# Expert tables split into fp16 halves during the mixers' heads and kept in DRAM: loaded ready, the first table by transposing DMAs, with the key roles exchanged

## The chip, the cores and the metric

The kernel runs on one core of one Trainium2 chip. The metric is the device time of one execution in microseconds (us); lower is better. Times of the kernel before are a median of 3 runs. The profile is one further execution, taken by the hardware profiler on the same program.

## The reference

One layer with two pre-norm sub-layers over 1024 latent tokens of 1024 channels; a prefix of 256 context tokens only feeds the start states. The first sub-layer is a pair of linear-attention mixers (8 HGRN heads and 4 GLA heads, both directions). The second is PEER, a product-key expert network of 128 x 128 = 16384 single-neuron experts:

```
q  = (tok @ wq).reshape(-1, 8, 2, 128)
s1 = einsum("nhd,kd->nhk", q[:, :, 0], k1)
s2 = einsum("nhd,kd->nhk", q[:, :, 1], k2)
v1, i1 = top_k(s1, 16)
v2, i2 = top_k(s2, 16)
top_s, top_c = top_k(v1[..., :, None] + v2[..., None, :], 16)
expert = i1[top_c // 16] * 128 + i2[top_c % 16]
gate = softmax(top_s)
act = gelu(einsum("pd,ped->pe", x, u[expert]))
out = einsum("pe,ped->pd", gate * act, v[expert])
```

Each token picks 16 experts in each of 8 heads. `u` and `v` are tables of 16384 rows of 1024 fp32 numbers (64 MiB each).

## The kernel before, in words

**Arithmetic.** TensorE works in fp16. Every large product is made of three: both operands are split into a high and a low fp16 half (`split`, lines 90 to 93: one ACT instruction writes the high half, one DVE instruction the low half), and `mm3` (lines 95 to 100) multiplies high by high, high by low and low by high, all added up in PSUM. All these matmuls show up under line 99; they are told apart by their output: `pj` (projections of the mixers), `pv` (their values by token), `pb` and `pso` (merge and output projection), `pq` (queries of the experts' keys), `ph` (u times the tokens), `pe` (activations times v).

**Order of the work.** The program is written out in full. A scheduler of the language orders each engine's instructions when the program is built: each engine then runs its own list strictly in order, and waits at the head of the list where an input is late. DMAs are issued from the lists of SP (`ld`: nearly all loads), ACT (`st_`: the stores) and POOL (the indirect gathers), in the same way.

**Stages.** First the modulation and norm, up to about 70 us of the profile. Then the mixers' *heads* (lines 299 to 682): `hg_proj`/`hg_scan` for 8 heads, `gla_proj`/`gla_scan` for 4, each loading 128 weight columns at a time through `slab` (line 165; three fp32 buffers `w32`), with the projections of the next head issued ahead of the scan of this one. In a scan DVE runs a chain of states (`R`, line 433) that PE feeds and reads. `merge_gate` and `modulation` (lines 611 and 621) fill in and close the heads. Then the merge and output projection (752 to 852), and then PEER.

**PEER.** Two of the eight blocks of 128 tokens do not go through all experts: `gathering` (line 864) fetches their chosen rows of u and v by indirect DMAs from POOL (line 892), 512 of them, and DVE uses each row (lines 871 and 876). The other 768 tokens go through all 16384 experts, in 128 tiles of 128. Tile `e` holds the experts `i * 128 + e`, so `i`, the first key, runs over the partitions. For each tile:

- `u_load` (line 902) loads 128 rows of u (512 KB fp32, `un`, two buffers);
- `u_turn` (line 907) transposes them with 8 PE transposes in fp32 against the identity into PSUM (`put`), ACT writes the high half (line 917) and a scaled fp32 copy (`uf`, line 919), POOL subtracts to the low half (line 920); the result `uT` has two buffers;
- `u_act` (line 925) multiplies with the tokens (48 matmuls into two PSUM tiles `ph`) and ACT takes the gelu;
- `weigh` (line 1078) multiplies with the gates on DVE and splits; `v_tile` (line 1087) loads 128 rows of v (`vn`, two buffers) and splits them on ACT and DVE (lines 92 and 93);
- `out_unit` (line 1094) multiplies four tiles' worth of activations with v (`pe`) and DVE adds the result to `acc`.

48 of the 128 tiles are *early* (line 123): their `u` part runs during the product-key stage (`prep`, line 1025: `route`, `choosing`, `gate_block`) and is kept in DRAM (`act_d`). The other 80 are *live*, and run in the expert stage, between 2880 and 4510 us of the profile. The gates are made by `gate_block` (line 995) from one-hot rows and kept in DRAM as `G_d`, with the first key ahead of the second. Two marks hold DVE's and POOL's order: `vmark` puts the use of a gathered row behind the last named DVE instruction (line 869), `pace` puts a gather's issue behind the last POOL subtraction of `u_turn`:

```
G.tensor_tensor(out=lo, in0=uf, in1=hi, op=ALU.subtract)
with tc.issue_after(pace[0].ins):
    G.indirect_dma_start(out=row, out_offset=None, in_=src[0], ...)
```

Of the kernel before, what the change touches and what calls it, by code (L numbers as in the profile page):

```python
# [8 lines left out]
F32 = mybir.dt.float32  # L9
# [9 lines left out]
P = 128  # L19
# [12 lines left out]
# powers of two that keep the low halves of split operands out of fp16's subnormals  # L32
# [30 lines left out]
AHEAD = 4  # L63


@with_exitstack
def tile_layer(ctx: ExitStack, tc: tile.TileContext, x, c, ctxt, c_ctx, ada_w, ada_b, norm_mix_g,
# [58 lines left out]
    # activations by feature: the mixers' input first, the experts' input later  # L126
# [5 lines left out]
    def rms_cols(tiles, pl, tag):  # L132
        """1 / rms of each row of the tiles"""
# [9 lines left out]
    def norm_T(tiles, ss, dst, sc, sh, pl, pp, tag, rows_of=None):  # L143
        """normalised rows, by feature, with a gain and a shift per feature, split in two"""
# [18 lines left out]
    # ================================================================ mixers  # L163
    with ExitStack() as mixers:
        def slab(src, c0, nm, sc, pool_lo=False):
            """128 columns of a weight, split"""
# [15 lines left out]
        # ---------------------------------------------------------- modulation and norm  # L182
        with ExitStack() as sa:
# [40 lines left out]
            # lower bounds: softmax over the two layers, first entry: 1/2 + 1/2 tanh of half the difference;  # L224
            # columns: (1 + lb) / 2, (1 - lb) / 2, -(1 - lb) / 2
# [10 lines left out]
            # normalised rows by feature  # L236
# [56 lines left out]
        # tokens in three ranges: context, first half, second half  # L293
# [4 lines left out]

        def proj(w16, r, nm, pp, m=P):
# [899 lines left out]
```

## Time and profile before

| | |
|---|---|
| median of 3 runs | 4614.6 us (4611.57 to 4617.51) |
| profiled execution, span from first to last instruction | 4615.8 us |
| TensorE (PE) busy | 4416.1 us, 96% of the span |
| VectorE (DVE) busy | 2794.3 us, 61% |
| ScalarE (ACT) busy | 1519.0 us, 33% |
| GpSimd (POOL) busy | 1459.2 us, 32% |
| TensorE's granted clock, mean | 0.969 of full speed |
| DMA | 709.58 MB, mean 154 GB/s |

For the profiled execution no time besides its span is given; the span lies inside the three runs' times. Busy shares are means over stages that differ. What a change in a stage is worth is read in that stage: which engine has no idle time there, and what it waits for. Transfers count as DMA share: the mean busy share of the core's 16 DMA engines.

### The profile page before, as it was taken

To read this page: it belongs to the slowest core of one execution; us is meant where nothing else is said; L and a number is where in the kernel's file an instruction comes from. 1 tells how busy PE (TensorE), PEld (TensorE's weight loads), DVE (VectorE), ACT (ScalarE), POOL (GpSimd) and SP (SyncE) were. 2 spreads that over 40 slices of the span, in tenths; PEclk is the share of its full clock that TensorE was granted. 3 is DMA by queue.
4 is the path that set the end of the run, shared out by engine and by line. 5 is a ranking of instruction groups with operands and counts; after the bars stand their busy time and mean duration, and the time that the engine had idled before them with its cause. 6 is when DMAs were issued, how large, how long until landed. Compare 5 with 4: busy or idle time off the path is not lost.

```text
span 4615.8 us, 61540 instructions
## 1 busy us (share of the span) xinstructions
PE 4416.1 (96%) x24821; PEld 2509.4 (54%) x24821; DVE 2794.3 (61%) x4946; ACT 1519.0 (33%) x2251; POOL 1459.2 (32%) x1077
## 2 busy tenths in 40 slices
PE   7999999999999989899989999999999999999998
PEld 3666566566554444455555555555555555455554
DVE  5434544334564486656985443677777776877777
ACT  6333432322332222343334433322222222222222
POOL 2111111100110345523543111444444444444442
PEclk9999999999999999799998988999999999999999
DMA  4111111101147532224433435767777776777775
GB/s 165 37 33 38 42 38 33 46 27 43 42 121 231 193 117 78 84 100 148 137 130 131 149 140 178 235 230 264 253 255 251 236 253 230 256 252 258 246 248 199
DMA packets 421019, 709.58 MB, mean 154 GB/s; under 512 B 22031, under 2 KB 286714, under 8 KB 416638
## 3 DMA queue, kind: packets, MB, share of 16 engines
q1 hardware_dynamic: 219812, 291.35, 19.4%
q0 software_dynamic: 73728, 268.47, 17.7%
q10 hardware_dynamic: 127194, 145.83, 9.3%
q8 instruction: 195, 3.19, 0.3%
q14 instruction: 90, 0.74, 0.1%
HBM read 610.14 MB, written 95.43 MB: 153 GB/s over the span
## 4 chain that ended last, share of the span: by engine, by line
PE 71%; DVE 12%; ACT 6%; DMA 4%; issue 4%; POOL 3%; ACTq 0%; SPq 0%; DVEq 0%; POOLq 0%
PE pe L99 16%; PE ph L99 15%; PE pgm L1010 8%; ACT gs L1012 3%; PE pj_f0h L99 2%; PE pv_h L99 2%; PE pv_g L99 2%; PE pj_f1h L99 2%; PE pj_m L99 2%; PE pj_qh L99 2%; PE put L913 2%; PE pj_gh L99 1%; PE pq L99 1%; PE pso L99 1%; PE pj_kg L99 1%
## 5 line engine op out<-in xcount | busy, mean ns | idle before, releaser
L99 PE MATMUL ph<-hb,uT 128*128 128x256 f16 (+1 forms) x6144 | 1094.7, 335 | 5.1 <-ACT ac L933 2.6
L99 PE MATMUL pe<-v,w 128*128 128x512 f16 x4608 | 1013.0, 380 | 18.9 <-DVE acc L1102 13.3
L99 PEld LDWEIGHTS <-uT 128*128 128x128 f16 x6144 | 619.3, 101 | 409.4 <-issue 34.1
L99 PEld LDWEIGHTS <-w 128*128 128x128 f16 x4608 | 451.2, 98 | 567.3 <-issue 20.0
L920 POOL TENSOR_TENSOR uT<-uf,uT 128x512 f16<-128x512 f32 x256 | 361.0, 1420 | 476.1 <-ACT uf L919 474.2
L892 POOL DMA_INDIRECT row_False<-in_peer_u_dram,idx x256 | 303.2, 1185 | 459.1 <-DVE row_False L871 410.2
L892 POOL DMA_INDIRECT row_True<-in_peer_v_dram,idx x256 | 296.7, 1159 | 452.1 <-DVE gacc L876 406.3
L871 DVE SCALAR_TENSOR_TENSOR row_False<-row_False,h2n 128x1024 f32<-128x1024 f32 x256 | 345.0, 1354 | 139.0 <-DMA row_False<-in_peer_u_dram,idx 139.0
L1010 PE MATMUL pgm<-oh 128*128 128x128 f16 x1536 | 391.2, 410 | 37.9 <-ACT gs L1012 31.2
L876 DVE SCALAR_TENSOR_TENSOR gacc<-row_True,dots,gacc 128x1024 f32<-128x1024 f32 x254 | 356.2, 1402 | 1.6
L88 DVE TENSOR_TENSOR oh<-iota,rTr 128x1024 f16<-128x1024 f16 x192 | 151.8, 827 | 325.8 <-PE pgm L1010 325.8
L1012 ACT ACTIVATE gs<-pgm 128x512 f32<-128x512 f32 x192 | 204.8, 1067 | 419.0 <-PE pgm L1010 418.9
L1010 PEld LDWEIGHTS <-oh 128*128 128x128 f16 x1536 | 223.5, 146 | 179.0 <-issue 64.2
L933 ACT ACTIVATE ac<-ph 128x256 f32<-128x256 f32 (+1 forms) x256 | 125.3, 494 | 441.2 <-PE ph L99 434.1
L1102 DVE TENSOR_TENSOR acc<-pe,acc 128x512 f32<-128x512 f32 x372 | 252.9, 686 | 15.1 <-PE pe L99 15.0
L92 ACT ACTIVATE v<-vn 128x1024 f16<-128x1024 f32 x128 | 135.0, 1057 | 337.9 <-DMA vn<-in_peer_v_dram 222.5
L917 ACT ACTIVATE uT<-put 128x512 f16<-128x512 f32 x256 | 153.5, 600 | 272.3 <-PE put L913 264.2
L93 DVE SCALAR_TENSOR_TENSOR v<-vn,v 128x1024 f16<-128x1024 f32 x128 | 177.2, 1392 | 72.9 <-ACT v L92 68.5
L99 PE MATMUL pj_m<-hb,w_m 128*128 128x512 f16 x768 | 186.1, 399 | 2.2 <-DVE lf_g L85 1.6
L99 PE MATMUL pq<-hb,w_wq 128*128 128x512 f16 x768 | 180.7, 384 | 4.5 <-POOL w_wq L88 3.0
L99 PEld LDWEIGHTS <-hb 128*128 128x128 f16 x1536 | 150.3, 98 | 17.3
L919 ACT ACTIVATE uf<-put 128x512 f32<-128x512 f32 x256 | 154.9, 605 | 11.8 <-issue 7.6
(360 smaller groups left out, 5948.0 us busy)
## 6 DMA issues: line engine op xcount, KB each, us to landing
un<-in_peer_u_dram SPq DMA_DIRECT2D x128, 512.0 KB
vn<-in_peer_v_dram SPq DMA_DIRECT2D x128, 512.0 KB
G_d<-gs ACTq DMA_DIRECT2D x24, 2048.0 KB
gt<-G_d ACTq DMA_DIRECT2D x32, 1536.0 KB
act_d<-ac ACTq DMA_DIRECT2D x48, 384.0 KB
acr<-act_d SPq DMA_DIRECT2D x48, 384.0 KB
mw<-in_ada_w_dram SPq DMA_DIRECT2D x32, 512.0 KB
w_wq<-in_peer_wq_dram SPq DMA_DIRECT2D x32, 512.0 KB
```

Of the source, the lines that this page charges most:

```text
L88: eng.tensor_tensor(out=out, in0=in0, in1=in1, op=op)
L93: return V.scalar_tensor_tensor(out=lo, in0=src, scalar=float(scale), in1=hi, op0=ALU.mult, op1=ALU.subtract)
L99: PE.matmul(ps, lhsT=a(k), rhs=b(k), start=n == 0, stop=n == last)
L871: V.scalar_tensor_tensor(out=row, in0=row, scalar=1.0, in1=h2n, op0=ALU.mult, op1=ALU.mult, accum_out=dots[:, s:s + 1])
L876: V.scalar_tensor_tensor(out=gacc[n], in0=row, scalar=dots[:, s:s + 1], in1=gacc[n], op0=ALU.mult, op1=ALU.add)
L892: G.indirect_dma_start(out=row, out_offset=None, in_=src[0], in_offset=bass.IndirectOffsetOnAxis(ap=gsel[n][0][:, s:s + 1], axis=0))
L917: S.activation(hi, pv, AF.Copy, scale=SU)
L919: S.activation(uf, pv, AF.Copy, scale=SU)
L920: pace[0] = G.tensor_tensor(out=lo, in0=uf, in1=hi, op=ALU.subtract)
L1010: PE.matmul(pgm[:, t, :], lhsT=oh[:, 0, :, t1 + t], rhs=oh[:, j, :, t1 + t], start=j == 2, stop=j == 3)
L1012: S.activation(gs[:, :, q0:q0 + 4].rearrange("p i n -> p n i"), pgm, AF.Copy, scale=SA / SG)
L1102: vmark[0] = V.tensor_tensor(out=acc[n][:, hs], in0=ps, in1=acc[n][:, hs], op=ALU.add)
```

## The change

1. **Presplit.** During the heads a generator `presplit` loads each tile of u and v in halves of 512 columns (256 KB, tile `pin`, three buffers), splits it on ACT and DVE (tile `pout`, three buffers, both fp16 halves), and stores it in two new DRAM tensors, `u_d` and `v_d`: 512 such jobs, loads and stores both on SP's queue. `meanwhile`, called after every projection of 512 columns, issues three jobs (`PRE = 3.0`).
2. **u.** `un`, the PE transposes, `put`, `uf` and the POOL subtraction are gone. `u_load` now issues two transposing DMAs from `u_d` straight into `uT` (three buffers in place of two).
3. **v.** `v_tile` loads both fp16 halves from `v_d`; its split is gone.
4. **Keys exchanged.** Tile `e` now holds the experts `e * 128 + p`, 128 neighbouring rows; the second key runs over the partitions. `gate_block` swaps the two one-hot factors, so `G_d` has the second key ahead.
5. **Besides.** PSUM's `ph` tiles have two buffers each; gathers are no longer held behind `pace`; the tail's `x1` rows use v's buffers; the scratch for GpSimd's DMA descriptors is set to 4096 bytes of a partition. Comments and docstrings are removed, which shifts the line numbers.

```
+        def presplit():
+            jobs = [(w, e, hf) for e in range(NKEY) for w in range(2) for hf in range(2)]
+            ins, outs = [], []
+            def load():
+                w, e, hf = jobs[len(ins)]
+                t = hs_.tile([P, HD], F32, name=f"pin{w}_{e}_{hf}", tag="pin", bufs=3)
+                ld(out=t, in_=(v_r if w else u_r)[e, :, hf * HD:(hf + 1) * HD])
+                ins.append(t)
+            def store():
+                w, e, hf = jobs[len(outs) - 1]
+                cs = slice(hf * HD, (hf + 1) * HD)
+                ld(out=v_d[e][:, :, cs] if w else u_d[e][:, :, cs].rearrange("a p d -> p a d"), in_=outs[-1])
+            load()
+            load()
+            for n, (w, e, hf) in enumerate(jobs):
+                if len(ins) < len(jobs):
+                    load()
+                o = hs_.tile([P, 2, HD], F16, name=f"pout{w}_{e}_{hf}", tag="pout", bufs=3)
+                split(ins[n], o[:, 0], o[:, 1], SV if w else SU)
+                if outs:
+                    store()
+                outs.append(o)
+                yield
+            store()
+        def meanwhile(w):
+            owed_[0] += PRE * w
+            while owed_[0] >= 1.0:
+                owed_[0] -= 1.0
+                next(ahead, None)
...
     def u_load(e):
-        un = pu.tile([P, D], F32, name=f"un{e}", tag="un", bufs=2)
-        ld(out=un, in_=u_r[:, e, :])
-        return un
-    def u_turn(e, un, early):
...
+        uT = pu.tile([P, 2, KC, P], F16, name=f"uT{e}", tag="uT", bufs=3)
+        for j in range(2):
+            nc.sync.dma_start_transpose(out=uT[:, j], in_=u_d[e][j])
         return uT
...
-            ph = ppu.tile([P, HT - o], F32, name=f"ph{hf}_{e}", tag=f"ph{hf}")
+            ph = ppu.tile([P, HT - o], F32, name=f"ph{hf}_{e}", tag=f"ph{hf}", bufs=2)
...
-                tt(V, oh[:, 0], iota, col(0), ALU.is_equal)
-                tt(V, oh[:, 1], iota, col(1), ALU.is_equal)
+                tt(V, oh[:, 0], iota, col(1), ALU.is_equal)
+                tt(V, oh[:, 1], iota, col(0), ALU.is_equal)
...
     def v_tile(e):
-        vn = pd.tile([P, D], F32, name=f"vn{e}", tag="vn", bufs=2)
-        ld(out=vn, in_=v_r[:, e, :])
         v16 = pd.tile([P, 2, D], F16, name=f"v16_{e}", tag="v16", bufs=2 * GR)
-        vmark[0] = split(vn, v16[:, 0], v16[:, 1], SV)
+        ld(out=v16, in_=v_d[e])
         return v16
```

**How the order moves.** The rows that follow are the lists that the engines run, in order; a name's letters are the tile, the figures after it its number and place.

SP's list in the heads, six rows before. Each loads 128 columns of a mixer's weight (`w32_...`, `q`, `g`, `f0`, `f1` for queries, gate and the two forget gates of a head):

```order
L168 DMA w32_qh3_2487<-in_w_in_dram 128x8x128
L168 DMA w32_gh2_2675<-in_w_in_dram 128x8x128
L168 DMA w32_f0h4_2874<-in_w_in_dram 128x8x128
L168 DMA w32_f1h4_2958<-in_w_in_dram 128x8x128
L168 DMA w32_qh4_3042<-in_w_in_dram 128x8x128
L340 DMA w32_vh40_3101<-in_w_in_dram 128x8x128
```

The same list with the change, 11 rows ahead of a weight load and one behind it (`pin0` and `pout0` are of u, `pin1` and `pout1` of v, then the tile's number and the half):

```order
L317 DMA pin0_31_0_3258<-in_peer_u_dram 128x512
L323 DMA u_d_82<-pout0_30_1_3254 128x2x512
L317 DMA pin0_31_1_3290<-in_peer_u_dram 128x512
L323 DMA v_d_83<-pout1_30_0_3260 256x1x512
L317 DMA pin1_31_0_3296<-in_peer_v_dram 128x512
L323 DMA v_d_83<-pout1_30_1_3292 256x1x512
L317 DMA pin1_31_1_3302<-in_peer_v_dram 128x512
L323 DMA u_d_82<-pout0_31_0_3298 128x2x512
L317 DMA pin0_32_0_3470<-in_peer_u_dram 128x512
L323 DMA u_d_82<-pout0_31_1_3304 128x2x512
L175 DMA w32_qh4_3932<-in_w_in_dram 128x8x128
L317 DMA pin0_32_1_3476<-in_peer_u_dram 128x512
```

Between two weight loads SP's list now has 0 to 26 jobs' loads and stores, each behind the split that frees or fills its buffer. In ACT's list the last of the 512 splits stands ahead of the fourth of the five evictions of the last GLA head's values (`pv_g`).

DVE's list during a chain of states, before:

```order
L433 SCALAR_TENSOR_TENSOR R_h4_0_0_4108<-R_h4_0_0_4108,gam_h4_0_3927,u0_h4_0_0_4118 128x128
L433 SCALAR_TENSOR_TENSOR R_h4_0_1_4113<-R_h4_0_1_4113,gam_h4_1_3976,u1_h4_0_0_4119 128x128
L433 SCALAR_TENSOR_TENSOR R_h4_0_0_4108<-R_h4_0_0_4108,gam_h4_0_3927,u1_h4_0_0_4119 128x128
L433 SCALAR_TENSOR_TENSOR R_h4_0_1_4113<-R_h4_0_1_4113,gam_h4_1_3976,u0_h4_0_0_4118 128x128
L433 SCALAR_TENSOR_TENSOR R_h4_0_0_4108<-R_h4_0_0_4108,gam_h4_0_3927,u0_h4_0_0_4118 128x128
```

And with the change, the end of one group of eight steps, the splits behind it and the next step:

```order
L484 SCALAR_TENSOR_TENSOR R_h2_0_0_3538<-R_h2_0_0_3538,gam_h2_0_3321,u1_h2_0_4_3585 128x128
L484 SCALAR_TENSOR_TENSOR R_h2_0_1_3543<-R_h2_0_1_3543,gam_h2_1_3370,u0_h2_0_4_3584 128x128
L94 SCALAR_TENSOR_TENSOR pout1_37_0_4009<-pin1_37_0_3969,pout1_37_0_4009 128x512
L94 SCALAR_TENSOR_TENSOR pout1_37_1_4015<-pin1_37_1_3975,pout1_37_1_4015 128x512
L94 SCALAR_TENSOR_TENSOR pout0_38_0_4021<-pin0_38_0_4007,pout0_38_0_4021 128x512
L484 SCALAR_TENSOR_TENSOR R_h2_0_0_3538<-R_h2_0_0_3538,gam_h2_0_3321,u0_h2_0_6_3602 128x128
```

One to three splits stand between groups of eight steps of the chain, which PE feeds group by group.

SP's list in the expert stage, before (`un` and `vn` are tiles of u and v, `acr` the kept activations of an early tile):

```order
L1089 DMA vn40_26452<-in_peer_v_dram 128x1024
L904 DMA un42_26509<-in_peer_u_dram 128x1024
L1131 DMA acr38_26252<-act_d_81 128x768
L1089 DMA vn41_26583<-in_peer_v_dram 128x1024
L904 DMA un43_26649<-in_peer_u_dram 128x1024
L1131 DMA acr40_26450<-act_d_81 128x768
```

And with the change:

```order
L1162 DMA acr36_27745<-act_d_81 128x768
L956 DMA_TRANSPOSE uT41_27976<-u_d_82 128x8x128 x2
L1122 DMA v16_36_27747<-v_d_83 128x2048
L1122 DMA v16_37_27857<-v_d_83 128x2048
L1122 DMA v16_38_27922<-v_d_83 128x2048
L1122 DMA v16_39_28032<-v_d_83 128x2048
L1162 DMA acr38_27920<-act_d_81 128x768
L956 DMA_TRANSPOSE uT42_28150<-u_d_82 128x8x128 x2
```

A live tile's pair of transposing DMAs stands up to two live tiles ahead of the one in use, and the four v tiles of a group follow one another. On PE's list the 1024 transposes are gone, on POOL's the 256 subtractions, and on ACT's and DVE's the 128 splits of v; ACT also loses the 512 copies out of `put`.

## Rows read from the trace of the kernel before

**Rows 1.** The page's head and first part: span; busy us, share, instructions of an engine.

```profile
span 4615.8 us, 61540 instructions
...
PE 4416.1 (96%) x24821; PEld 2509.4 (54%) x24821; DVE 2794.3 (61%) x4946; ACT 1519.0 (33%) x2251; POOL 1459.2 (32%) x1077
```

**Rows 2.** Stages: from:to length, busy of PE, PEld, DVE, ACT, POOL, PEclk, DMA share, GB/s.

```profile
70.00:1130.00 1060.00, 1037.33 (x7147) 666.19 (x7148) 460.67 (x791) 387.27 (x557) 147.22 (x80) 0.99 0.14 38
1130.00:1480.00 350.00, 327.42 (x1968) 186.08 (x1967) 178.02 (x290) 107.81 (x155) 35.05 (x17) 0.95 0.37 115
1480.00:1867.00 387.00, 354.58 (x1657) 166.06 (x1655) 237.94 (x815) 102.98 (x140) 157.65 (x106) 0.97 0.42 134
1867.00:2880.00 1013.00, 951.37 (x4788) 574.86 (x4789) 613.77 (x1536) 399.85 (x573) 343.58 (x246) 0.91 0.38 134
2880.00:4510.00 1630.00, 1610.12 (x8649) 856.65 (x8649) 1192.74 (x1373) 452.32 (x716) 741.71 (x595) 1.00 0.75 248
4510.00:4616.00 106.00, 90.81 (x465) 45.44 (x462) 85.92 (x93) 29.37 (x49) 29.36 (x23) 0.95 0.57 191
```

**Rows 3.** Groups by line, whole span: busy us, mean ns | idle before, releaser.

```profile
L920 POOL TENSOR_TENSOR uT<-uf,uT 128x512 f16<-128x512 f32 x256 | 361.0, 1420 | 476.1 <-ACT uf L919 474.2 <-issue 0.3
...
L93 DVE SCALAR_TENSOR_TENSOR v<-vn,v 128x1024 f16<-128x1024 f32 x128 | 177.2, 1392 | 72.9 <-ACT v L92 68.5 <-issue 4.4
...
L913 PE MATMUL put<-ident,un 128*128 128x128 f32 x1024 | 142.2, 278 | 0.0
...
L92 ACT ACTIVATE v<-vn 128x1024 f16<-128x1024 f32 x128 | 135.0, 1057 | 337.9 <-DMA vn<-in_peer_v_dram 222.5 <-PE pe L99 106.6 <-PE put L913 8.4
```

**Rows 4.** Groups by line on PE in the expert stage, 2880 to 4510 us.

```profile
L99 PE MATMUL pe<-v,w 128*128 128x512 f16 x4305 | 947.1, 380 | 18.9 <-DVE acc L1102 13.3 <-ACT w L1083 5.2 <-DVE w L1084 0.4
L99 PE MATMUL ph<-hb,uT 128*128 128x512 f16 (+1 forms) x3720 | 620.5, 327 | 2.6 <-ACT ac L933 2.6
L913 PE MATMUL put<-ident,un 128*128 128x128 f32 x624 | 81.0, 273 | 0.0
```

**Rows 5.** Timeline of the expert stage on PE, one live tile: start us, length us.

```profile
3471.40 1.04 PE L913 MATMUL put<-ident,un 128*128 128x128 f32 x8
...
3472.27 7.96 PE L99 MATMUL ph<-hb,uT 128*128 128x256 f16 x48
```

**Rows 6.** Tile yT, split from SBUF: ns min/median/max, first and last start us.

```profile
L92 ACT ACTIVATE yT<-msg_g x16: 612/629/642, 1485.8 to 1801.6; 128x512 f16<-128x512 f32 x16
L93 DVE SCALAR_TENSOR_TENSOR yT<-msg_g,yT x16: 667/689/2121, 1486.5 to 1802.2; 128x512 f16<-128x512 f32 x16
```

**Rows 7.** Tiles pj_f0h and v_g: first and last start of heads' projections.

```profile
L99 PE MATMUL pj_f0h<-hc,w_f0h x192: 272/273/421, 73.6 to 646.9; 128*128 128x256 f16 x192
...
L351 ACT ACTIVATE v_g<-pv_g x20: 597/597/598, 747.1 to 1164.5; 128x512 f32<-128x512 f32 x20
```

**Rows 8.** Tile un: SP's time to issue one load, ns min/median/max.

```profile
L904 SPq DMA_DIRECT2D un<-in_peer_u_dram x128: 327/328/742, 1867.1 to 4498.0; - x128
```

**Rows 9.** DMA queues in 3200 to 3400 us: packets, MB, share of 16 engines.

```profile
q1 hardware_dynamic: 4176, 14.42, 19.5%
q10 hardware_dynamic: 12352, 6.29, 12.0%
```

**Rows 10.** The same for 70 to 1130 us: ACT's queue, mostly stores of y.

```profile
q10 hardware_dynamic: 6592, 7.34, 2.0%
```

**Rows 11.** A 512 KB load and ACT's wait for it, and its stretch's stage row.

```profile
1450.03 0.38 SPq L168 DMA_DIRECT2D w_bg<-in_w_branch_gla_dram  x1
...
1454.41 1.06 ACT L92 ACTIVATE w_bg<-w_bg 128x1024 f16<-128x1024 f32 x1 [7.37 <-DMA w_bg<-in_w_branch_gla_dram]
...
1420.00:1480.00 60.00, 54.56 (x256) 25.44 (x255) 27.15 (x29) 12.67 (x16) 0.00 (x0) 0.94 0.85 274
```

More of the change, by code (lines that the diff above doesn't have):

```diff
@@ L63 @@
 AHEAD = 4
+PRE = 3.0
 @with_exitstack
@@ L124, in tile_layer @@
     act_d = dram.tile([len(early), P, TD], F32, name="act_d")
+    u_d = dram.tile([NKEY, 2, P, D], F16, name="u_d")
+    v_d = dram.tile([NKEY, P, 2, D], F16, name="v_d")
+    u_r = peer_u[0].rearrange("(e p) d -> e p d", p=NKEY)
+    v_r = peer_v[0].rearrange("(e p) d -> e p d", p=NKEY)
     hb = [const.tile([P, 2, KC, HT], F16, name=f"hb{i}") for i in range(2)]
@@ L297, in tile_layer @@
         DS = 1.0 / (SH * SW)
+        hs_ = pool(heads, "hs", reuse_waits="tile")
+        HD = D // 2
+        def presplit():
[22 more added lines that the diff above has]
+            store()
+        ahead = presplit()
+        owed_ = [0.0]
+        def meanwhile(w):
[3 more added lines that the diff above has]
+                next(ahead, None)
         def proj(w16, r, nm, pp, m=P):
@@ L675, in tile_layer @@
             pass
+        for _ in ahead:
+            pass
         if "yhg" in dbg:
@@ L890, in gathering @@
                     row = pq.tile([P, D], F32, name=f"row{n}_{s}_{hh is None}", tag="row", bufs=AHEAD)
-                    with tc.issue_after(pace[0].ins):
-                        G.indirect_dma_start(out=row, out_offset=None, in_=src[0],
-                                             in_offset=bass.IndirectOffsetOnAxis(ap=gsel[n][0][:, s:s + 1], axis=0))
+                    G.indirect_dma_start(out=row, out_offset=None, in_=src[0],
+                                         in_offset=bass.IndirectOffsetOnAxis(ap=gsel[n][0][:, s:s + 1], axis=0))
                     held.append((n, s, row, hh, dots))
@@ L902, in u_load @@
     def u_load(e):
-        un = pu.tile([P, D], F32, name=f"un{e}", tag="un", bufs=2)
-        ld(out=un, in_=u_r[:, e, :])
-        return un
-    def u_turn(e, un, early):
-        uT = pu.tile([P, 2, KC, P], F16, name=f"uT{e}", tag="uT", bufs=2)
-        for q in range(2):
-            pt = ppu.tile([P, 512], F32, name=f"put{e}_{q}", tag="put", bufs=2)
-            for k in range(4):
-                PE.transpose(pt[:, k * P:(k + 1) * P], un[:, (q * 4 + k) * P:(q * 4 + k + 1) * P], ident)
-            pv = pt.rearrange("p (a b) -> p a b", a=4)
-            hi, lo = uT[:, 0, q * 4:q * 4 + 4, :], uT[:, 1, q * 4:q * 4 + 4, :]
-            if early:
-                S.activation(hi, pv, AF.Copy, scale=SU)
-                uf = pu.tile([P, 4, P], F32, name=f"uf{e}_{q}", tag="uf", bufs=2)
-                S.activation(uf, pv, AF.Copy, scale=SU)
-                pace[0] = G.tensor_tensor(out=lo, in0=uf, in1=hi, op=ALU.subtract)
-            else:
-                split(pv, hi, lo, SU)
+        uT = pu.tile([P, 2, KC, P], F16, name=f"uT{e}", tag="uT", bufs=3)
+        for j in range(2):
+            nc.sync.dma_start_transpose(out=uT[:, j], in_=u_d[e][j])
         return uT
@@ L1044, in early_tile @@
             pend = next(es, None)
-            uTn = u_turn(pend, u_load(pend), True) if pend is not None else None
+            uTn = u_load(pend) if pend is not None else None
             ac = u_act(e, uT)
@@ L1107, in tile_layer @@
     live = [e for e in range(NKEY) if e not in early]
-    uT = u_turn(live[0], u_load(live[0]), True)
+    uT = u_load(live[0])
     li = 0
```

17 lines of the change are left out of this document (8 added, 9 removed).

## The prediction, made before the change was run

> **What bounds the kernel now.** I read the page's head first: PE is busy for 4416.1 of 4615.8 us [rows 1]. That share says little by itself, so I cut the span into its stages [rows 2] and read, in each, what PE leaves idle: 22.7 us of the 1060 in which the heads project, 61.6 of the 1013 with the product keys, 19.9 of the 1630 of the expert stage. No other engine comes near in a stage: DVE has 43% in the heads and 73% in the expert stage. So PE sets the end nearly everywhere, and time that PE is spared counts in full, as long as nothing else becomes late. DMA is the other column to look at: 0.14 busy at 38 GB/s in the heads, 0.75 at 248 GB/s in the expert stage. The change moves load from where DMA is busy to where it is idle. The groups by line [rows 3] price what it removes, and the groups of the expert stage [rows 4] show what PE waits for there.
>
> **The change, part by part.**
>
> *PE transposes of u: -142 us.* All 1024 `put` matmuls go. They hold PE for 142.2 us in all and have no idle time before them [rows 3]; for one tile they are a block of 1.04 us ahead of the 7.96 us of its first `ph` matmuls [rows 5]. 81.0 us of it lie in the expert stage [rows 4], the other 61.2 in the key stage, where PE is 94% busy too. I take all of it.
>
> *Waits of PE in the expert stage: -11 us.* PE waits 18.9 us at `pe`, mostly for DVE's sums, and 2.6 at `ph` for ACT [rows 4]. DVE is rid of the 177.2 us that split v, ACT of the 135.0 for the same [rows 3], and `ph` has a second buffer. What is left is DVE's order between gathered rows and sums, so I take half of 21.5; the bounds are 0 and 21.5.
>
> *POOL's subtractions, 361.0 us [rows 3], and ACT's copies out of `put`: 0.* They lie beside PE and PE does not wait for them. Gathers lose the hold behind `pace`, but a row buffer still becomes free only when DVE has used the row: 0. The key exchange keeps the number and shape of the one-hots: 0. Loads of v have the same 512 KB, now without a split behind them: 0. The tail gets more buffers for `x1`: 0, since PE is still summing there. The smaller descriptor scratch serves four gathers in flight, as before: 0; if it held them back, DVE's slack of 27% in the expert stage is the cover.
>
> *The presplit in the heads: +45 us.* 512 jobs are added, each with an ACT and a DVE instruction on 128x512 from SBUF. The nearest rows are those of `yT`, the same form: 629 and 689 ns [rows 6]. That is 322 us of ACT and 353 us of DVE. The order puts the first job behind the first projection (73.6 us) and the last one just ahead of the end of the last GLA head's values (1164.5 us) [rows 7]: some 1080 us, one job in 2.11 us. DVE goes from 43% to some 77% there, ACT from 37% to some 67%. On the queues: 1024 more DMAs on SP at 0.33 us to issue [rows 8] are 338 us, beside few others. For the engines of DMA, a load costs what q1 shows, 19.5% of 200 us for 14.42 MB [rows 9], 2.7 us per MB, so 0.71 us for 0.262 MB; a store costs what ACT's queue shows in the heads, 2.0% of 1060 us for 7.34 MB [rows 10], 0.76 us. Together 1.47 in 2.11 us is 0.70, beside the 0.14 of now: 0.84 busy.
>
> What can hurt is the loop through three buffers: split done, SP issues the next load, it lands, ACT, DVE. Where DMA is 0.85 busy, a 512 KB load takes 4.4 us from its issue to ACT's start [rows 11]; 256 KB should take 0.7 less. 3.7 + 0.63 + 0.69 is 5.0 us, so 1.7 us per job, below the 2.11 that PE leaves. If each job waits in ACT's and in DVE's list for one instruction of 128x1024 (1.06 and 1.39 us [rows 3]), and the load takes the full 4.4, it is 8.2 us or 2.7 per job: 512 jobs then last 1400 us, +315. That is the upper bound. Below zero nothing is possible, as nothing leaves the heads. With half of such waits the loop takes 6.2 us, 2.07 per job: it just fits on the mean and will bind in spells. A job that is late holds ACT's list, and so the evictions that PE needs. What PE idles where DVE has 73% is 1.2%, where it has 61% in short chains 8.4% [rows 2]. I take 4% more of 1080, 45 us, between them.
>
> *The transposing DMAs: 0.* Before shows none, so I bound them. The expert stage will last 1630 - 81 - 11 = 1538 us for 80 live tiles, 19.2 us each, and the order has a pair issued up to two live tiles ahead; so a pair that takes its time alone is hidden up to 19.2 us. For the DMA engines the bound is lower. They are busy for 0.75 x 1630 = 1222 us, of which 80 loads of `un` take 1.42 us each at q1's price, 113. This leaves 1538 - 1109 = 429 us, 5.4 us per tile. Lower bound of a pair: the plain load, 1.4 us. Nearest row for small pieces: ACT's queue in the expert stage with 12352 packets of some 510 bytes in 12.0% of 200 us [rows 9], 31 ns each. If a pair is read in pieces of 256 bytes, 2048 of them at that price are 4.0 us. I take 4.0: the share comes to 0.93, and PE is still not held. The upper bound has no near row; were each 32 bytes written at a packet's price, a pair would take 32 us and hold everything.
>
> The Trainium skill, "DMA: Bandwidth & Descriptors", in its table of latencies and measured facts, gives transposing DMAs 261 GB/s where the middle dimension is not contiguous; that would be 2.0 us per tile and the same sum.
>
> Sum: 4615.8 - 142 - 11 + 45 = 4508 us. The span lies 1.2 us above the runs' median and inside the three runs, so I carry it over as it is: **4508 us**, 2.3% faster. A measurement of this kernel can tell some 0.2%, 9 us, from no change.
>
> **The rivals.**
>
> *Transposes bound the expert stage (slower, 0.15).* For it: DMA is already 0.75 busy there, and the price has no row. Against: the bytes stay the same, and a pair has 5.4 us of all engines. At 8 us, twice the piece price, the stage lasts 1109 + 640 = 1749 us in place of 1630. Then the time is 4615.8 - 61 + 45 + 119 = 4719. It decides from 5.4 us on. If instead the 16 blocks of 128x128 of a pair pass one after another, it decides from 19.2 us per pair, 1.2 us per block; at a tenth above, 20.9 us, the stage lasts 1672 and the time is 4642. The Trainium skill speaks for this way: "VectorE: DVE Perf Modes", section "The three transpose paths", has 1309 ns for a 128x128 block by DMA against 390 on TensorE, and 16 such blocks in turn would be 20.9 us, so 4642; no run so far shows it.
>
> *The job loop bounds the heads (slower, 0.13).* For it: SP's list puts each weight load behind the jobs ahead of it, so PE can't run away from them. Against: the sum of the parts, 5.0 us, against 6.3. At 7.5 us per round, 512 jobs last 1280 us, 200 more than now: 4615.8 - 153 + 200 = 4663. It makes the whole slower than before from 7.3 us on.
>
> *Half of PE's gain is lost (faster, but less, 0.12).* In the key stage DVE's top-16 chains and one-hots may be what a sparer PE then waits for, and its granted clock is 0.91 in that stage [rows 2], so a new wait may cost clock. For it: the idle 61.6 us of that stage. Against: early tiles still fill in. 4615.8 - 71 - 5 + 45 = 4585.
>
> That the change doesn't do what it says is excluded by the order: the transposes, the subtractions and the splits are gone from the lists.
>
> **How the numbers follow.** My forecast has 0.60, its own range 4450 (no cost in the heads, all waits gone) to 4560 (twice the cost). The rivals have 0.15, 0.13 and 0.12. For 8 in 10 the range goes from 4445 to 4690: below it is 0.05, above it the dearer half of the transposes' case and of the loop's, some 0.12. Faster by over 0.2%: nearly all of the forecast's case and of the third rival, 0.70. Slower: 0.24, nearly all of the first two. Within 0.2%: 0.06.
>
> **What would show it.** Right: no `put` on PE, PE's idle time in the expert stage below 25 us and that stage near 1540 us long; the first merge matmul some 45 us later than now; DVE near 77% and DMA near 0.84 in the heads. Wrong: PE waiting for `uT` behind a DMA (first rival); ACT's `pout` splits waiting for `pin` loads and the last of them later than 1300 us (second); PE's idle time in the key stage grown by 60 us or more (third). I would be wrong altogether if a pair of transposes takes more than 5.4 us of all the DMA engines.

## The result: 2.6% slower, and the profile after

The changed kernel takes 4737.0 us (median of 4 runs, 4731.3 to 4742.7), beside 4616.1 for the kernel before on the same chip: a ratio of 1.0257, 95% interval 1.0243 to 1.0272. The forecast was 4508, its range up to 4690. Slower was given 0.24.

The page of the kernel after, its head and PE's share of the first part, against [rows 1]:

```profile
span 4740.8 us, 61763 instructions
...
PE 4370.4 (92%) x23797; PEld 2422.2 (51%) x23797; DVE 2867.2 (60%) x5330; ACT 1437.4 (30%) x2123; POOL 1067.5 (23%) x821
```

PE is busy for 46 us less, though 1024 transposes are gone, and its share falls from 96% to 92%. I cut both spans where the program changes from one stage to the next: the heads up to the last GLA scan, then from the first merge matmul to the first `pe`, then to the end. The stages of the kernel before, cut so (from:to length, busy of PE, PEld, DVE, ACT, POOL, PEclk, DMA share, GB/s):

```profile
70.00:1290.00 1220.00, 1190.35 (x8133) 760.15 (x8134) 533.39 (x920) 450.65 (x646) 173.50 (x94) 0.98 0.14 39
1478.30:2890.40 1412.10, 1315.60 (x6486) 745.34 (x6485) 857.92 (x2357) 508.25 (x719) 501.23 (x352) 0.93 0.40 135
2890.40:4615.80 1725.40, 1692.98 (x9080) 898.42 (x9080) 1272.91 (x1459) 477.33 (x759) 771.07 (x618) 0.99 0.74 245
```

And of the kernel after:

```profile
70.00:1515.00 1445.00, 1243.13 (x8127) 786.87 (x8128) 876.37 (x1431) 742.16 (x1156) 173.19 (x93) 0.94 0.71 218
1706.40:3106.60 1400.20, 1308.92 (x6233) 716.47 (x6232) 803.99 (x2348) 414.79 (x526) 375.67 (x256) 0.90 0.47 134
3106.60:4740.80 1634.20, 1600.98 (x8309) 813.27 (x8309) 1054.80 (x1340) 194.56 (x312) 504.45 (x458) 0.99 0.88 260
```

The reader is to see two things. The heads take 1445 us in place of 1220; PE has the same number of matmuls in them (8127 and 8133), but 172 us more idle time (202 against 30) and 53 us more busy time at a granted clock of 0.94 in place of 0.98. Behind the heads the kernel is faster, by 12 us up to the first `pe` and by 91 behind it. The stretch between the heads and the first merge matmul (188 and 191 us) hardly changes. In one number each: the first merge matmul comes at 1706.4 us in place of 1478.3, 228 later; from there to the end it takes 3034.4 in place of 3137.5, 103 less. 228 - 103 = 125 is the whole difference of the two spans.

What PE waits for in the heads (chief rows of the waits of PE, 70 to 1515 us: total us, times, longest):

```profile
PE kt_h L443 <- ACT kn_h L438: 53.7, 8, 9.9
PE py_g L644 <- ACT v_g L401: 18.5, 5, 5.5
PE pv_g L100 <- ACT v_g L401: 15.5, 10, 2.2
PE pv_h L100 <- ACT v_h L401: 14.5, 9, 3.1
PE pj_f1h L100 <- ACT at_f0h L581: 9.8, 3, 8.6
```

Over all rows of that view, PE waits 166.9 us for ACT, where it waited 19.6 before. ACT is only half busy. What it waits for itself (waits of ACT, same stretch):

```profile
ACT pout L93 <- DMA u_d<-pout: 242.9, 163, 14.8
ACT pout L93 <- DMA v_d<-pout: 207.4, 156, 4.3
```

For 450 us ACT stands at the head of its list before a job's split, because the store that reads the output buffer `pout` has not landed. The timeline shows how this reaches PE (ACT, and then PE, 500 to 520 us: start us, length us):

```profile
509.54 0.63 ACT L93 ACTIVATE pout<-pin 128x512 f16<-128x512 f32 x1 [1.18 <-DMA u_d<-pout]
512.65 0.63 ACT L93 ACTIVATE pout<-pin 128x512 f16<-128x512 f32 x1 [2.49 <-DMA v_d<-pout]
513.98 0.63 ACT L93 ACTIVATE pout<-pin 128x512 f16<-128x512 f32 x1 [0.70 <-DMA v_d<-pout]
514.52 0.58 ACT L401 ACTIVATE v_h<-pv_h 128x512 f32<-128x512 f32 x1
...
506.62 5.40 PE L100 MATMUL pv_h<-wv_h,hb 128*128 128x256 f16 x48 [0.56 <-ACT q_h L573]
515.15 5.10 PE L100 MATMUL pv_h<-wv_h,hb 128*128 128x256 f16 x30 [3.13 <-ACT v_h L401]
```

PE ends a group of `pv_h` at 512.02 us, and ACT could empty that PSUM tile at once. But two splits stand ahead of the eviction `v_h`, each behind a store; ACT comes to it at 514.52, and PE goes on at 515.15, after 3.13 us of waiting. The longest waits, at `kt_h`, have the same form: ahead of the copy `kn_h` (out of PSUM too) that ends the one of 9.9 us at 929.12, ACT's list has four splits from 922.40 to 927.69. The chain of waits from 500 to 520 us holds no PE at all (start us, length us):

```profile
511.29 6.31 DMA u_d<-pout
...
517.70 0.64 ACT pout L93
...
518.37 0.70 DVE pout L94
...
519.09 0.33 SPq L317
...
519.46 3.42 DMA v_d<-pout
```

Store, ACT's split, DVE's, SP's issue of the next load (L317, behind which the store stands in SP's list), store: the loop through `pout`. Its stores take 3.4 to 6.3 us from issue to release here.

### The profile page after: what moved, and what is told of

The parts are those of the page before. It is cut to its first block, busy times and chain, and to the rows that moved or that the text cites. A ratio compares the mean times of both kernels' runs of the same rounds, so it can differ in the third digit from the quotient of the medians.

```text
span 4740.8 us, 61763 instructions
## 1 busy us (share of the span) xinstructions
PE 4370.4 (92%) x23797; PEld 2422.2 (51%) x23797; DVE 2867.2 (60%) x5330; ACT 1437.4 (30%) x2123; POOL 1067.5 (23%) x821
## 4 chain that ended last, share of the span: by engine, by line
PE 49%; DMA 15%; issue 14%; DVE 13%; ACT 5%; POOL 2%; SPq 1%; ACTq 0%; DVEq 0%; POOLq 0%
PE pe L100 19%; PE ph L100 14%; DMA u_d<-pout 6%; DMA v_d<-pout 5%; PE pgm L1044 3%; DVE pout L94 2%; PE pj_m L100 2%; ACT pout L93 2%; PE pso L100 1%; PE pb_h L100 1%; SPq L317 1%; PE pb_g L100 1%; PE pq L100 1%; DMA mw<-in_ada_w_dram 1%; DMA w_wq<-in_peer_wq_dram 1%
## 5 line engine op out<-in xcount | busy, mean ns | idle before, releaser
L100 PE MATMUL ph<-hb,uT 128*128 128x256 f16 (+1 forms) x6144 | 1112.8, 339 | 0.0
L100 PE MATMUL pe<-v,w 128*128 128x512 f16 x4608 | 1012.1, 380 | 20.8 <-DVE w L1117 14.0
L94 DVE SCALAR_TENSOR_TENSOR pout<-pin,pout 128x512 f16<-128x512 f32 x512 | 371.1, 733 | 398.2 <-ACT pout L93 397.8
L942 POOL DMA_INDIRECT row_False<-in_peer_u_dram,idx x256 | 288.3, 1126 | 953.9 <-DVE row_False L922 901.7
L93 ACT ACTIVATE pout<-pin 128x512 f16<-128x512 f32 x512 | 319.0, 628 | 517.4 <-DMA u_d<-pout 242.9
L942 POOL DMA_INDIRECT row_True<-in_peer_v_dram,idx x256 | 281.4, 1099 | 603.9 <-DVE gacc L927 533.7
L927 DVE SCALAR_TENSOR_TENSOR gacc<-row_True,dots,gacc 128x1024 f32<-128x1024 f32 x254 | 324.7, 1278 | 36.1 <-DMA row_True<-in_peer_v_dram,idx 34.5
L922 DVE SCALAR_TENSOR_TENSOR row_False<-row_False,h2n 128x1024 f32<-128x1024 f32 x256 | 309.8, 1222 | 33.2 <-DMA row_False<-in_peer_u_dram,idx 32.9
L89 DVE TENSOR_TENSOR ac<-ac,gt 128x768 f32<-128x768 f32 x80 | 76.5, 957 | 257.8 <-ACT ac L967 257.8
L100 PEld LDWEIGHTS <-w_m 128*128 128x128 f16 x768 | 77.3, 103 | 103.7 <-issue 30.2
L100 PEld LDWEIGHTS <-w_wq 128*128 128x128 f16 x768 | 77.2, 101 | 93.2 <-issue 8.0
```

The costliest lines, as they stand in the source:

```text
L89: eng.tensor_tensor(out=out, in0=in0, in1=in1, op=op)
L100: PE.matmul(ps, lhsT=a(k), rhs=b(k), start=n == 0, stop=n == last)
L922: V.scalar_tensor_tensor(out=row, in0=row, scalar=1.0, in1=h2n, op0=ALU.mult, op1=ALU.mult, accum_out=dots[:, s:s + 1])
L927: V.scalar_tensor_tensor(out=gacc[n], in0=row, scalar=dots[:, s:s + 1], in1=gacc[n], op0=ALU.mult, op1=ALU.add)
L942: G.indirect_dma_start(out=row, out_offset=None, in_=src[0], in_offset=bass.IndirectOffsetOnAxis(ap=gsel[n][0][:, s:s + 1], axis=0))
```

## The experiments

One table first, from the profiles: the place of the last split, the first merge matmul (`pb_h`), the time from there to the end of the span, and the run's time (a median where there are more: before, after, e4, e7, e11 and e12; the others are single runs). The first column of figures gives the number of splits and the start of the last. Runs 1 to 12 stand beside the kernel before on other chips, where its median was 4620 to 4629 us; the ratios below are to those.

| kernel | splits, last at us | first `pb_h` at us | from there to the end | time us |
|---|---|---|---|---|
| before | none | 1478.3 | 3137.5 | 4616.1 |
| after | 512, 1390 | 1706.4 | 3034.4 | 4737.0 |
| e1_few_jobs | 4, 97 | 1488.7 | 3033.1 | 4523.5 |
| e2_out2 | 512, 1753 | 1790.2 | 3038.0 | 4829.9 |
| e3_out5 | 512, 1348 | 1711.6 | 3042.4 | 4755.7 |
| e4_u_only | 256, 790 | 1621.2 | 3048.4 | 4655.7 |
| e5_split_only | 512, 676 | 1544.7 | 3034.1 | 4580.5 |
| e6_dma_only | 3, 81 | 1506.3 | 3035.3 | 4543.3 |
| e7_u_paced | 256, 1394 | 1515.1 | 3038.4 | 4559.7 |
| e8_paced_all | 512, 1580 | 1685.4 | 3033.6 | 4720.7 |
| e9_put_twice | none | 1471.5 | 3234.7 | 4707.9 |
| e10_plain_u | 512, 1393 | 1710.6 | 3015.2 | 4727.6 |
| e11_u_spread | 256, 1535 | 1548.1 | 3043.8 | 4593.3 |
| e12_u_140 | 256, 1431 | 1518.5 | 3057.3 | 4572.8 |

The part behind the heads is the same code in after, e1, e2, e5, e6 and e8, but for the tile that e1 and e5 load (e3's two `w32` buffers reach into the merge); there it takes 3033 to 3038 us, so some 5 us of that column are scatter.

**1. The jobs left out.**

```
- jobs = [(w, e, hf) for e in range(NKEY) for w in range(2) for hf in range(2)]
+ jobs = [(w, e, hf) for e in range(1) for w in range(2) for hf in range(2)]
  (and uT and v16 of every tile loaded from u_d[0], v_d[0])
```

> Only the four jobs of tile 0 are done, and all 128 tiles load tile 0's halves: the later stages have the same loads and matmuls, the heads are rid of 508 jobs (the output is not the reference's). Theory A (the jobs alone lengthen the heads, and the later stages stand for themselves): the first merge matmul back at 1478 us, and 4740.8 - 228 = 4513 us in all. Rival (the later stages still suffer from the jobs, or part of the loss in the heads is not theirs): first merge matmul later than 1500 us, or the stages behind it shorter by over 20 us than the 3034 us of the changed kernel.

The first merge matmul came at 1488.7 us, and behind it 3033.1 us. So 218 of the 228 us belong to the 508 jobs left out, and the stages behind don't feel them. The two halves of the result can be treated apart. The last 10 us lie in the four jobs that stayed. The fourth split needs the first one's `pout`, and the mixers' eviction `at_f0h` stands behind it (ACT twice, then PE: start us, length us):

```profile
97.28 0.63 ACT L93 ACTIVATE pout<-pin 128x512 f16<-128x512 f32 x1 [14.24 <-DMA u_d<-pout]
97.82 0.58 ACT L581 ACTIVATE at_f0h<-pj_f0h 128x512 f32<-128x512 f32 x1
...
98.45 12.68 PE L100 MATMUL pj_f1h<-hb,w_f1h 128*128 128x512 f16 x48 [8.23 <-ACT at_f0h L581]
```

One late store (DVE came to its half of the first split only at 91.21 us) costs PE 8.23 us here, and its last `pj_f0h` comes at 670.2 us in place of 659.9.

**2 and 3. Fewer and more buffers `pout`.** My first theory (A) was that the three `pout` buffers set the pace, as the chain suggests.

```
- tag="pout", bufs=3
+ tag="pout", bufs=2        (e2)
+ tag="pout", bufs=5        (e3; and tag="w32", bufs=3 -> 2 for the space)
```

> Two buffers pout in place of three. Theory A (the loop through pout bounds the heads: a store of some 5.1 us, ACT 0.63, DVE 0.69, issue 0.8, together 7.2 us): 3.6 us per job, the last split at some 1900 us, and 4740 + 530 = 5270 us in all. Theory B (the DMA engines, 0.76 busy, set the pace with their transfers): 2.5 to 2.8 us per job as now, under 4850 us. Theory C (ACT and DVE are too full, each job holds their lists): as B.

> Five buffers pout in place of three, paid for by w32 with two buffers in place of three. Theory A: the pout loop takes 7.2/5 = 1.4 us per job, and the pin loop, 5.0/3 = 1.7, is next; both are below the 2.11 that PE leaves, so the heads lose under 100 us in place of 228: below 4610 us. Theory B: the engines have the same bytes, so 4700 us or more. Theory C: the splits take the same time of ACT and DVE, so 4700 us or more. Should two w32 buffers hold PE's weights up, PE's idle time shows pj and pv waiting for w32 loads.

Both missed A. Two buffers cost 84 us at the first merge matmul where it asked for 530 in the whole, five gained nothing. The pace of the jobs did follow the buffers in e2, 3.27 us a job (80.2 to 1753.1 us), not far from A's 3.6; PE's loss did not, as the order put fewer jobs beside the heads: 414 of the 512 splits come before the last GLA values, which end only 16 us later (1407.2 against 1391.3). In e3 ACT no longer waits for stores, but for loads (waits of ACT, 70 to 1400 us):

```profile
ACT pout L93 <- DMA pin<-in_peer_u_dram: 208.6, 138, 5.5
ACT pout L93 <- DMA pin<-in_peer_v_dram: 174.2, 128, 8.5
```

383 us at `pin` in place of 450 at `pout`: the other buffer of the same loop takes over at once. The loads are as long as the stores (chain of waits, 495 to 540 us: start us, length us, the shortest and the longest):

```profile
502.57 4.21 DMA pin<-in_peer_v_dram
...
522.73 6.28 DMA pin<-in_peer_u_dram
```

The loss of PE up to the last projection `pj_f0h`, which stands at 659.9 us before, hardly depends on the buffers: 795.2 after, 791.8 with two, 798.0 with five. (What two `w32` buffers cost by themselves was not run.)

**4. Only u.**

```
- jobs = [(w, e, hf) for e in range(NKEY) for w in range(2) for hf in range(2)]
+ jobs = [(w, e, hf) for e in range(NKEY) for w in range(1) for hf in range(2)]
- PRE = 3.0
+ PRE = 1.5
  def v_tile(e):
      ...
-     ld(out=v16, in_=v_d[e])
+     vn = pd.tile([P, D], F32, name=f"vn{e}", tag="vn", bufs=2)
+     ld(out=vn, in_=v_r[e])
+     vmark[0] = split(vn, v16[:, 0], v16[:, 1], SV)
```

> Only u is split ahead (256 jobs, three per two projections); v is loaded in fp32 and split by ACT and DVE in the expert stage as in the kernel before. Theory A: the loop takes 2.4 us per job where 4.2 are to be had, so it binds only in spells: the first merge matmul within 40 us of before, the later stages as with the change within 10 us, 4515 to 4560 us. Rival (v's splits, 177 us of DVE and 135 of ACT in the expert stage, come back onto PE's path): that stage 11 us or more longer than with the change. Theory C (each job blocks lists): half of the loss stays, first merge matmul at some 1590 us, 4625 us.

Half the jobs, and still 143 us lost in the heads; ratio to before 1.0060 (1.0043 to 1.0077). The tile's row shows why (ACT's splits: ns min/median/max, first and last start us):

```profile
L93 ACT ACTIVATE pout<-pin x256: 612/629/634, 80.0 to 790.2; 128x512 f16<-128x512 f32 x128
```

The 256 jobs end at 790 us, one per 2.8 us, not one per 4.2 over the whole of the heads. The number of jobs per projection in the program does not set their place: the order puts them as early as their buffers seem to allow. Up to 790 us this kernel loses as much as the full change, behind it nothing: its last `pj_f0h` comes at 802.6 us and its last GLA values at 1307.9, each 143 us later than before. That made theory D: not the jobs' cost counts, but that ACT's list holds a split before its data can be there, and stands still with the evictions behind it.

**5 and 6. Splits without DMAs, DMAs without splits.**

```
e5:  if len(ins) < 4: load()   split(ins[min(n, 3)], ...)   if 1 <= n <= 4: store()
e6:  if n < 3: o = hs_.tile(...); split(ins[n], ...)   else: o = outs[n % 3]
     (e5 also loads uT and v16 of every tile from u_d[0], v_d[0])
```

> All 512 pairs of splits on ACT and DVE stay, but only tile 0's four jobs load and store: the others split tiles that are there already and store nothing (output not the reference's). Theory C (the splits' own time on ACT and DVE, 640 + 700 ns a job, holds what PE waits for): most of the 228 us stays, first merge matmul after 1600 us. Theory D (ACT's list, and DVE's behind it, stands still at a split whose DMA is late, and the evictions behind it hold PE): the waits are gone, first merge matmul before 1540 us.

> All 512 loads and stores stay, but only three splits are made, and the stores write those three tiles again and again (output not the reference's). Theory B (the DMA engines' load itself delays the weights, the mixers' stores and with them PE): most of the loss stays, first merge matmul after 1600 us. Theory D: nothing on ACT or DVE waits for these DMAs, so first merge matmul before 1540 us, however busy the engines are.

Against the 1488.7 us of e1, the splits alone cost 56 us, though they crowd into 79 to 676 us; e5 has e1's wait of PE at the fourth job too (7.8 us). e6 has no fourth split and not this wait, so it is set against the kernel before: the DMAs alone cost 28 us (1506.3 against 1478.3), with the DMA engines full (stage row of e6):

```profile
500.00:900.00 400.00, 389.12 (x2707) 252.79 (x2706) 151.40 (x259) 137.71 (x200) 43.91 (x24) 1.00 1.00 330
```

Together they cost 228. So 144 us belong to neither, if the two parts simply add up: what is left are the waits that only arise where a split depends on a DMA. PE's waits for ACT in the heads, 147 us more than before, are of that size. e5 fell between the two bounds (1544.7 where D asked for less than 1540), so theory C keeps a share.

**7. Only u, and each split behind an eviction.** The same work as e4, in another place of the list:

```
+ with tc.issue_after(ev[0].ins) if ev[0] is not None else nullcontext():
      split(ins[n], o[:, 0], o[:, 1], SV if w else SU)
  (ev[0]: the last eviction of pj or pv on ACT traced so far)
```

> As e4_u_only, but each job's split on ACT stands behind the last eviction written ahead of it in the program, so the 256 jobs spread over the heads, one per 4.2 us, in place of filling their first 720 us at one per 2.8 us. Theory D: the loop of DMAs then has time to spare, ACT hardly waits for it, first merge matmul at 1480 to 1530 us, and 50 to 100 us faster than the kernel before. Theory C: the same number of splits costs the same, 140 us in the heads, 0.5 to 1% slower than before, as e4_u_only. Between: first merge matmul at 1530 to 1580, within 1% of before.

Ratio to before **0.9871 (0.9855 to 0.9888)**, 4559.7 us: faster than both kernels, by 1.3% against the one before. Of ACT's 1995 instructions in the trace the last of the 256 splits is the 994th, in e4 the 635th; they now come one per 5.1 us. ACT's waits in e7, 70 to 1515 us:

```profile
ACT at_f0h L583 <- PE pj_f0h L100: 91.2, 21, 14.5
ACT v_g L403 <- PE pv_g L100: 76.6, 20, 4.1
ACT pout L93 <- DMA u_d<-pout: 36.4, 24, 9.0
```

And in e4:

```profile
ACT pout L93 <- DMA u_d<-pout: 272.9, 172, 13.5
```

36.4 us in place of 272.9, and ACT now waits for PE, as it should where PE is the bound. The number of splits, their durations and their bytes are those of e4; their place, and with it their pace, makes 106 us at the first merge matmul. (The profile of e4 is of the longest of its four runs, that of e7 of the shortest; the medians differ by 96 us.) The runs also show what v's half of the presplit is worth: e4, e7, e11 and e12, which split v in the expert stage as before, take 3038 to 3057 us behind the heads, 4 to 23 more than the full change. For that, 256 of the 512 jobs were put on the heads.

**8. The whole change paced.** The edit of e7 on the changed kernel, with all 512 jobs.

> The whole change (512 jobs, u and v) with each split on ACT behind the last eviction ahead of it in the program, as in e7_u_paced. Theory D: what counts is the spare time of the loop, and there is none: 2.1 us per job are to be had, the loop takes 2.6, so the heads still end 150 to 230 us late and the time is 4670 to 4750 us. Rival (the place of the splits in the lists is what counts, not their number): first merge matmul before 1580 us and less than 4620 us.

1685.4 and 4720.7 us, within what D asked for: pacing gains 21 us at the first merge matmul where the loop has no time to spare. With 512 jobs it has none, with 256 it has.

**9. The price of the transposes.** In the kernel before:

```
- for k in range(4):
+ for k in (0, 1, 2, 3, 0, 1, 2, 3):
      PE.transpose(pt[:, k * P:(k + 1) * P], un[...], ident)
```

> The kernel before, with each of the 1024 transposes put made twice over (same result). Theory E (a block of 8 costs what the next matmul starts later, 0.85 us, as its last matmuls overlap with the next): 128 x 0.85, some 109 us longer than before. Rival (the 142 us of the group's busy time, 1.04 us a block plus what the slower clock adds): 140 us or more. Below 90 us something else waits there.

The run took 4707.9 us, 88 more than the median of before on its chip: less than the 109 of E, and under its bound of 90. In the profiles 97 us more lie behind the first merge matmul, which came 7 us sooner though nothing had changed ahead of it. The timeline gives the block itself (PE: start us, length us):

```profile
3526.69 1.91 PE L913 MATMUL put<-ident,un 128*128 128x128 f32 x16
3528.43 7.96 PE L99 MATMUL ph<-hb,uT 128*128 128x256 f16 x48
```

16 transposes put the next `ph` 1.74 us after their start, the 8 of before 0.87 (3471.40 to 3472.27 in [rows 5]): 128 x 0.87 = 111 us. PE's busy time behind the first merge matmul rose by 110 us (3008.6 to 3118.7), and 14 us of it came back, as PE's waits at `pe` fell from 18.9 us [rows 4] to 5.3. The stage rows of this run, cut as above:

```profile
1471.50:2928.20 1456.70, 1361.18 (x6877) 792.70 (x6876) 861.74 (x2359) 516.30 (x724) 494.25 (x352) 0.93 0.39 132
2928.20:4706.20 1778.00, 1757.54 (x9714) 966.90 (x9712) 1254.85 (x1457) 476.61 (x756) 762.64 (x618) 1.00 0.72 237
```

**10. Plain loads in place of the transposing ones.**

```
- nc.sync.dma_start_transpose(out=uT[:, j], in_=u_d[e][j])
+ ld(out=uT[:, j], in_=u_d[e][j].rearrange("p (k q) -> p k q", k=KC))
```

> The changed kernel with plain loads of the same 512 KB per tile from u_d in place of the transposing DMAs (uT then holds u untransposed, so the output is not the reference's). If the transposing DMAs are hidden: within 10 us of the changed kernel, 4730 to 4750 us, and only the DMA share of the expert stage falls, by 0.05 to 0.1 (3.1 against 1.4 us per pair). If they hold PE anywhere: more than 15 us faster.

The time, 4727.6 us, fell just below the band set for hidden DMAs. The part behind the heads took 3015.2 us, 18 less than the lowest of its kind and 19 less than in the kernel after, while the first merge matmul came 4 later: the transposing DMAs are nearly hidden, not wholly. The stage rows, cut as above:

```profile
1710.60:3104.00 1393.40, 1299.76 (x6233) 713.98 (x6232) 804.37 (x2348) 415.31 (x525) 375.16 (x256) 0.92 0.40 137
3104.00:4725.80 1621.80, 1602.03 (x8309) 814.05 (x8309) 1055.38 (x1340) 194.59 (x312) 505.66 (x458) 0.99 0.78 260
```

12 of the 19 us lie in the expert stage, all of it idle time of PE (19.8 us against 33.2), and most of that is one wait. In the kernel after it reads so (SP twice, DVE, PE: start us, length us):

```profile
3106.53 11.82 SPq L956 DMA_TRANSPOSE uT<-u_d x2
...
3119.08 0.38 SPq L1162 DMA_DIRECT2D acr<-act_d x1
...
3127.91 0.96 DVE L89 TENSOR_TENSOR acr<-acr,gt 128x768 f32<-128x768 f32 x1 [13.62 <-DMA acr<-act_d]
...
3129.79 12.75 PE L100 MATMUL pe<-v,w 128*128 128x512 f16 x50 [13.33 <-DVE w L1117]
```

A pair of transposing DMAs stands 11.82 us in SP's queue, and the load of an early tile's activations (`acr`) is issued only behind it; DVE waits for that load, and PE for DVE. The same wait, 13.4 to 15.6 us long, stands at the start of the expert stage in e1, e2, e3, e5, e6 and e8, and not in e10, where SP issues that `acr` load at 3107.70 us. The other 7 us lie in the stage up to the first `pe`, at a granted clock of 0.92 in place of 0.90; their cause is open.

SP's queue in the expert stage, 3400 to 3600 us, in the kernel after, and then in this one (packets, MB, share of 16 engines):

```profile
q1 hardware_dynamic: 24288, 15.99, 30.2%
```

```profile
q1 hardware_dynamic: 6048, 15.99, 21.6%
```

The same 15.99 MB with 20 DMAs for 10 tiles: (30.2 - 21.6)% of 200 us is 17.2 us, 1.7 per pair above the plain load's 1.4, so a pair takes an estimated 3.1 us of all the engines (3.6 by the DMA shares of the whole stage, 0.88 and 0.78).

**11 and 12. Two more spreads of e7.** 1.26 jobs per projection with the merge gates' evictions as marks too (e11); 1.4, and the left-over jobs ahead of the modulation (e12).

> As e7_u_paced, but 1.26 jobs per projection in place of 1.5, and the merge gates' evictions count as marks too, so that the jobs spread to the end of the modulation, one per 5.4 us. Theory D: fewer waits yet, first merge matmul 5 to 20 us sooner than the 1515 us of e7_u_paced, some 0.2 to 0.4% faster than that. Rival (the rest of e7_u_paced's loss is the splits' own time on ACT and DVE, which stays): the same within 5 us.

> As e7_u_paced with 1.4 jobs per projection in place of 1.5, and the some 17 jobs that are left over issued ahead of the modulation in place of behind it. Theory D: fewer waits in the heads (between the 28 us that e7_u_paced had lost by the last GLA projection and the 7 us of e11_u_spread), the left-over jobs beside the last GLA scan: first merge matmul at 1490 to 1515 us, ratio to before 0.983 to 0.987. Rival: the left-over jobs run in one row, 2 us each, and hold the merge, first merge matmul after 1520 us, ratio 0.988 or more.

Neither beat e7: ratios 0.9943 (0.9922 to 0.9964) and 0.9893 (0.9873 to 0.9913). Both missed what D asked for, 5 to 20 us sooner than e7 and 1490 to 1515 us at the first merge matmul, where they came at 1548.1 and 1518.5. e11 reaches the last GLA values at 1171 us, 7 behind the kernel before, so its thinner row costs next to nothing there. But what is left runs behind the modulation with nothing else to do (ACT's timeline, 1440 to 1550 us):

```profile
1528.74 0.63 ACT L93 ACTIVATE pout<-pin 128x512 f16<-128x512 f32 x1 [1.95 <-DMA u_d<-pout]
1530.55 0.63 ACT L93 ACTIVATE pout<-pin 128x512 f16<-128x512 f32 x1 [1.19 <-DMA u_d<-pout]
```

One split every 2 us, each behind a store, up to 1535 us: the bare loop of three buffers is 6 us long. In e12 the last splits stand in such rows too, up to 1432 us, with other work of ACT between them.

## Why the prediction was wrong

**The presplit, +45 us: wrong; it was +228.** This is the step that failed. I had the right mechanism in a sentence ("a job that is late holds ACT's list, and so the evictions that PE needs") and the wrong size in the next. First, the loop that I added up goes from the split through the next load; the store that frees `pout` is as long (3.4 to 6.3 us in the chain above) and I left it out, having priced the stores for the DMA engines only. The jobs took 2.56 us each (1311 us for 512), 7.7 per round of three, not 6.2. The store is not the whole of it: in run 3, where no split waits for a store, a round of the loads that I had added up took 7.4 us (1262 us for 512 jobs): a load took 4.2 to 6.3 us in the stretch shown, not 3.7. Secondly, I set PE's loss between two shares of idle time (1.2% and 8.4%) that other engines had caused; nothing tied them to this loop. The runs put in their place: 56 us for the splits, 28 for the DMAs, and 144 left for the waits between them. It is the second rival (0.13) that came, with 7.7 us per round where I had worked out 4663 us for 7.5. Its signs were right: `pout` splits late, the last of them at 1390 us, after 1300. Only ACT waited for stores rather than loads. As the heads grew longer than forecast, DVE came to 61% and DMA to 0.71 in them, not to 77% and 0.84.

**The transposes, -142 us: -111.** Group busy time counts a block to the end of its last matmul, and that overlaps the next. My own rows had it: in [rows 5] the `ph` matmuls start 0.87 us after the `put` block that is 1.04 us long. Run 9 confirms it: 0.87 us for 8 more, and 110 us more of busy time for 1024.

**PE's waits, -11 us: -3.** On PE the groups behind the first `pe` read now:

```profile
L100 PE MATMUL pe<-v,w 128*128 128x512 f16 x4608 | 1012.1, 380 | 20.8 <-DVE w L1117 14.0 <-DVE acc L1133 3.0 <-DVE acc L1131 2.2
L100 PE MATMUL ph<-hb,uT 128*128 128x512 f16 (+1 forms) x3701 | 614.4, 326 | 0.0
```

`pe` waits 20.8 us where it waited 18.9 [rows 4], `ph` no longer at all (5.1 in the whole span before). But one wait makes 13.3 of the 20.8, and the transposing DMAs bring it (run 10). Without them `pe` waits 13.3 us in all, so 11 of the 24.0 us of before (18.9 and 5.1) are gone, as forecast (what each freed engine gave was not taken apart). The transposing DMAs took most of that back.

**The transposing DMAs, 0: some 18 us.** Some 3.1 us per pair against the 4.0 that I took and the bound of 5.4; the stage's DMA share is 0.88, against the 0.93 of my sum. PE never waits for `uT`, so the first rival was wrong in both forms. What I did not ask is what else stands in SP's queue behind a pair: the `acr` load of run 10. The Trainium skill, "VectorE: DVE Perf Modes", section "The three transpose paths", gives 1309 ns for one 128x128 block by DMA; for the 16 blocks of a pair in turn that would be an estimated 20.9 us. The trace disagrees, with no wait at `ph`. The Trainium skill, "DMA: Bandwidth & Descriptors", section "Latency and other measured facts", by whose 261 GB/s a pair would be an estimated 2.0 us, was nearer to the measured 3.1.

**The third rival** (half of PE's gain lost in the key stage) was wrong as put: PE waits no longer there (its idle time from the first merge matmul to the first `pe` is 91 us in place of 97). That stage gained only 12 us because 139 of the live tiles' `ph` matmuls moved into it (2443 against 2304), some 23 us, and because its other matmuls took some 16 us longer, at a granted clock of 0.90 in place of 0.93.

Added up on PE behind the first merge matmul: busy time fell by 99 us (3008.6 to 2909.9), that is 110 for the transposes by run 9, less some 11 that the other matmuls took longer. Idle time fell by 4. Together -103, and with +228 the 4615.8 of before become 4740.8. Had only the heads' term been right, 4615.8 - 153 + 228 = 4691 would have been the forecast, and slower its sign.

## What to carry to other kernels

Work that is put "beside" a busy engine isn't free by its busy time alone: where engines run fixed lists, ask at each added instruction how long it can stand at the head of its list, and who is queued behind it. Walk every buffer of such a loop round, the output buffers through their stores too, compare the longest with the time there is per round, and if it has no time to spare, halve the work or pin it behind what the critical engine has already released; the same 256 jobs made the first merge matmul 143 us later than before, or 37, by their place in ACT's list. A queue that issues DMAs is such a list too: ask what stands behind a slow one. And take an instruction's price from the start of the next one on its engine, not from its group's busy time.

## What I had not expected of the hardware

With the DMA engines full (1.00 busy at 330 GB/s from 500 to 900 us) the heads ended only 28 us later (run 6). Where neither table's data is waited for, crowded DMA engines are cheap here; it is the wait that costs. And waits came with a second cost: with the same matmuls PE was busy 53 us longer in the heads, at a granted clock of 0.94 in place of 0.98, while it had 172 us more idle time between its groups.

A transposing DMA holds SP's queue three times as long as a plain one, 1.30 us where a plain load of the same 256 KB took 0.42 in run 10 (medians), and at times much longer (ns min/median/max, first and last start us):

```profile
L956 SPq DMA_TRANSPOSE uT<-u_d x256: 1232/1300/10580, 2097.4 to 4630.6; - x128
```

SP mostly has the time for it in the expert stage. Where it had not, the `acr` load behind it came late, and PE lost 13.3 us.
